# Two-input GpSimd work moved to VectorE, and Strassen sums accumulated in PSUM, in a hybrid SSD and attention layer

## The chip, the cores and the metric

The kernel runs on one core of a Trainium2 chip. Its time is the device time of one execution in microseconds (us). Engines are named as the profile names them: PE (matmul), DVE (VectorE), ACT (ScalarE), POOL (GpSimd) and SP, whose queue issues every DMA.

## The reference

One layer with two token mixers on a sequence of 1024 positions and a width of 1024, in float32. Shortened:

```python
ada = silu(c) @ w_ada + b_ada;  shift, scale, gate = split(ada, 3)
h = rmsnorm(x, norm_w) * (1 + scale) + shift
z_ssm, xbc, dt_raw, q, k, v, z_att, f_logit, g_logit = split(h @ w_in)   # 8472 columns
# SSD branch: 16 heads of 64, 2 groups, state 64, chunks of 128
xbc = silu(causal_conv(xbc, 4 taps));  xs, B, C = split(xbc)
dt = softplus(dt_raw + dt_bias);  a_cs = cumsum(-exp(a_log) * dt)  # inside a chunk
y = ((C B^T) * exp(a_cs[l] - a_cs[s]) masked) @ (xs * dt) + C @ state * exp(a_cs) + d_skip * xs
y_ssm = rmsnorm(y * silu(z_ssm), ssm_norm_w)
# attention branch: 8 heads of 128, causal
p = softmax(q k^T / sqrt(128) + f_cum[query] - f_cum[key]);  y_att = (p @ v) * silu(z_att)
g_ssm, g_att = split(sigmoid(g_logit + b_gate))
merged = g_ssm * (y_ssm @ w_proj_ssm) + g_att * (y_att @ w_proj_att)
out = rmsnorm(x + gate * (merged @ w_out), final_norm_w)
```

## The kernel before

**Split products.** Every float32 matrix A becomes two tiles of a matmul type, Ah (A rounded) and Al = A - Ah, and a product is three matmuls: Ah Bh, Ah Bl and Al Bh. `split` (L101 to L104) makes the pair: ACT casts (L102), then an engine given as an argument subtracts (L103). The default is GpSimd, `G`; some calls give `V`, VectorE. `unit` loads 128 x 512 weights into a tile `wr` and splits them into `wh` and `wl`. Operands called h or hh are high parts, l or hl low parts.

**Stages.** In order of time: normalisation of x, transposed into `hh`, `hl`, with DVE preparing what PE transposes (L261, L263, L302) and making the low part (L307); a first slab of v with the dt and forget columns (`t_slab`, L140 to L142; `tmp`, L348) and `t_forms`, which builds the Strassen forms of h (`tha`, `tla`, `thb`, `tlb`); then the pair stage; the SSD scan; attention; the projections of both branches; the output projection with the final normalisation.

**The pair stage.** `c_pair` computes two slabs of 128 columns of the in-projection at a time, 19 pairs, in Winograd's form of Strassen: sums of the four weight blocks (L476 to L479), seven splits f1 to f7, seven products of 12 matmuls of 512 columns (L495 to L497), each into a PSUM bank of its own from `bank()`, which goes round eight banks (three named `mm`, five `pp`). f1 is copied out (L503), and seven adds on DVE (L504, 505, 507, 508, 511, 514, 517) combine the products with tiles `pe`. What an evac does depends on the slab: `silu_out` (tanh on ACT, L524, then DVE, L525), `conv_out` (a copy, later DVE operations of 1024, L541 to L547), `gate_out` (tanh, L186). `w_sums` (L571 to L592) prepares Strassen sums of the projections' weights between pairs and stores them to `ws_scr`.

**SSD.** `ssd_half` handles four quarters of the heads by eight chunks. Per chunk: the decay matrix `ab` on ACT and DVE with its split into `m`, transposes of `xs` (L691), `xd` (L700), `xe` and their splits into `xr`, the state `sn` with its split, the products (L728, L739, L740) and the sums on DVE (L741). The squares of y collect in `sacc` (L777, L778). The rest of the v and some q and k slabs (L115 to L117, L140 to L142) are handed to the scheduler as work of lower priority.

**After the scan.** `sacc` is summed by PE (L784), raised to -1/2 by GpSimd (L789), transposed (L791). `attend` computes logits (L1012), softmax pieces (L1013 to L1021), transposes and p v; q and k are split in `qk_slab` at 1024 columns, v in `v_load`.

**Projections.** `prod_c` and `post` do each branch's projection in the same seven products, for four blocks p, with DVE adds as in the pairs; `b_form` builds the forms of the data. Three products of the SSD projection run as `early` work during attention. In the output projection `out_pre` (L1126) adds x1, u3 and u4 into the residual on GpSimd, and `out_done` adds the last product, squares, scales and stores. The tables `WV` and `WVI` give the weight splits of some blocks to DVE.

**Order.** A scheduler with a timeline model fixes the order of instructions on each engine when the kernel is built, from the order of the code and the priorities (`APRI`, `SPRI`). At run time every engine takes its own queue in order.

Of the kernel before, what the change touches and what calls it, by code (L numbers as in the profile page):

```python
# [31 lines left out]
P = 128  # L32
# [18 lines left out]
OSSM = (1, 2, 6, 7, 5, 4, 3)  # L51
OATT = (1, 2, 6, 7, 5, 4, 3)
OOUT = (1, 2, 6, 7, 5, 4, 3)
WV = {'ps': (), 'pa': (1,), 'o': (1, 2, 3)}
WVI = (("o", 3),)
# [14 lines left out]
def build(ctx, tc, t):  # L70
# [16 lines left out]
    def unit(src, n, eng=G):  # L87
# [13 lines left out]
    def split(raw, hi, lo, n, eng=G):  # L101
        A.copy(out=hi[:, :n], in_=raw[:, :n])  # L102
        eng.tensor_tensor(out=lo[:, :n], in0=raw[:, :n], in1=f32(hi[:, :n]), op=ALU.subtract)  # L103
        return hi, lo  # L104
# [91 lines left out]
    def w_in(n, i, p):  # L196
        if (n, i, p) in ws_scr:
            return unit(ws_scr[n, i, p], 512, V if p in WV[n] or (n, i) in WVI else G)
        return unit(t["w_" + n][p + 4 * (i == 4), i % 2 == 0 and 1 or 0], 512)
# [160 lines left out]
    with tc.tile_pool(name="pa", bufs=1, side="right") as pa, \  # L360
# [74 lines left out]
        def t_forms(k):  # L435
# [3 lines left out]
            for b, kk, hs, eng in ((b11, k, lo, V), (b12, k, hi, G), (b22, k + 4, hi, G), (b21, k + 4, lo, V)):  # L439
                eng.tensor_tensor(out=b, in0=f32(hh[kk][:, hs]), in1=f32(hl[kk][:, hs]), op=ALU.add)  # L440
# [4 lines left out]
            for b, th, tl, hs, eng in ((b11, th1, tl1, lo, V), (b12, th1, tl1, hi, G), (b22, th2, tl2, hi, V),  # L445
                                       (b21, th2, tl2, lo, G)):
# [12 lines left out]
        def c_pair(sa, sb, evac_a, evac_b):  # L459
# [22 lines left out]
            f6 = s_form(s2)  # L482
            f7 = a_form(a21)
            f5 = s_form(s1)
            f4 = a_form(a22)
            f2 = a_form(a12)
            f3 = s_form(s4)

            def prod(f, xs, k0, hf):
                ps = bank()  # L490
                hs = slice(hf * 512, (hf + 1) * 512)
                for k in range(4):
                    w = slice(k * P, (k + 1) * P)
                    xh, xl = xs[k0 + k]
                    PE.matmul(ps, lhsT=f[0][:, w], rhs=xh[:, hs], start=(k == 0), stop=False)  # L495
                    PE.matmul(ps, lhsT=f[0][:, w], rhs=xl[:, hs], start=False, stop=False)
                    PE.matmul(ps, lhsT=f[1][:, w], rhs=xh[:, hs], start=False, stop=(k == 3))  # L497
# [4 lines left out]
            x1, u2, u3, u4 = pe_tile(), pe_tile(), pe_tile(), pe_tile()  # L502
            A.copy(out=x1, in_=prod(f1, h, 0, 0))  # L503
# [71 lines left out]
        def w_sums(n, p, gb=None):  # L575

            def raw_in(sl, u):
                x = raw_tile()[:, :512]
                SP.dma_start(out=x, in_=t["w_" + n][sl, u])
                if gb is not None:  # L580
                    (V if u else G).tensor_tensor(out=x, in0=x, in1=gb[:, 512 * (sl // 4):512 * (sl // 4) + 512],
# [6 lines left out]
            G.tensor_tensor(out=a21, in0=a11, in1=a21, op=ALU.subtract)  # L588
            G.tensor_tensor(out=s4, in0=a12, in1=s2, op=ALU.subtract)
# [40 lines left out]
    with tc.tile_pool(name="sd", bufs=1, side="right") as sd, \  # L630
# [40 lines left out]
        def ssd_half(qd, hf, xs, ys, st32, sn):  # L671
# [3 lines left out]
            for c in range(4 * hf, 4 * hf + 4):  # L675
# [81 lines left out]
        for qd in range(4):  # L757
            st32, sn = sd.tile([P, 256], F32, tag="st32", bufs=1, name="st32"), None
            for hf in range(2):
# [7 lines left out]
                for i in range(2):  # L767
# [8 lines left out]
                    else:  # L776
                        A.activation(out=zt, in_=y, func=AF.Square)  # L777
                        G.tensor_tensor(out=sacc[:, hs], in0=sacc[:, hs], in1=zt, op=ALU.add)  # L778
# [75 lines left out]
    def b_t2(b11, b12, b22, b21=None):  # L854
# [5 lines left out]
        if b21 is not None:  # L860
            G.tensor_tensor(out=b21, in0=b21, in1=t2, op=ALU.subtract)
        return f

    RESULT = {2: (0, 0), 4: (1, 0), 3: (0, 1)}

    def post(i, p, ps, x, u3, done, pre=None):


        if i == 1:
            x[p] = fin_tile("x1", 4)  # L870
            A.copy(out=x[p], in_=ps)
        elif i == 6:
            V.tensor_tensor(out=x[p], in0=ps, in1=x[p], op=ALU.add)
        elif i in (5, 7):
            if p not in u3:
                u3[p] = fin_tile("u3", 4)
                if i == 5:
                    A.copy(out=u3[p], in_=x[p])
                    V.tensor_tensor(out=x[p], in0=ps, in1=x[p], op=ALU.add)
                else:  # L880
                    V.tensor_tensor(out=u3[p], in0=ps, in1=x[p], op=ALU.add)
                if pre:
                    pre(1, 1, p, (x if i == 5 else u3)[p])
            else:
                y, z = (u3, x) if i == 7 else (x, u3)
                V.tensor_tensor(out=y[p], in0=ps, in1=y[p], op=ALU.add)
                if not pre:
                    V.tensor_tensor(out=ps, in0=ps, in1=z[p], op=ALU.add)
                done(1, 1, p, ps)
        else:  # L890
            if not pre:
                V.tensor_tensor(out=ps, in0=ps, in1=u3[p] if i == 4 else x[p], op=ALU.add)
            done(*RESULT[i], p, ps)
        if pre and i in (1, 5, 7):
            pre(*RESULT[{1: 2, 5: 3, 7: 4}[i]], p, (u3 if i == 7 else x)[p])

    def prod_c(i, n, bf, x, u3, done):

        for p in range(4):
            hi, lo = w_in(n, i, p)  # L900
            ps = bank()
            for k in range(4):
                c = slice(k * P, (k + 1) * P)
                PE.matmul(ps, lhsT=hi[:, c], rhs=bf[k][0], start=(k == 0), stop=False)
                PE.matmul(ps, lhsT=hi[:, c], rhs=bf[k][1], start=False, stop=False)
                PE.matmul(ps, lhsT=lo[:, c], rhs=bf[k][0], start=False, stop=(k == 3))
            post(i, p, ps, x, u3, done)
# [14 lines left out]
    sx, su3 = {}, {}  # L922

    def early(i):

        fs = []
# [5 lines left out]
        for k in range(4):  # L932
            if i == 2:
                e = piece(4 + k, LO)
            elif i == 7:
                e = raw_tile()[:, :512]
                V.tensor_tensor(out=e, in0=ub[22][k], in1=ub[12][k], op=ALU.subtract)
            elif i == 3:
                e = ub[22][k]
            else:  # L940
                e = piece(k, LO)
                for q in {1: (), 5: (12,), 6: (12, 22), 4: (12, 22)}[i]:
                    V.tensor_tensor(out=e, in0=ub[q][k], in1=e, op=ALU.subtract)
                if i == 4:
                    e2 = piece(4 + k, LO)
                    V.tensor_tensor(out=e, in0=e2, in1=e, op=ALU.subtract)
            fs.append(b_split(e))
# [6 lines left out]
        prod_c(i, "ps", fs, sx, su3, done)  # L954

    with tc.tile_pool(name="at", bufs=1, side="right") as at, \
# [97 lines left out]
        for h in range(AH):  # L1054
# [10 lines left out]
            for i in EARLY.get(h, ()):  # L1065
                early(i)
                if i == 1:
# [9 lines left out]
    with tc.tile_pool(name="finp", bufs=1, space=PSUM) as fpp_:  # L1077
# [4 lines left out]
        b = {**ub, **(b_quads(us_scr, (11, 21)) if 4 not in done_early else {})}  # L1082
# [3 lines left out]
        prep_u = 6 in done_early  # L1086
# [154 lines left out]
```

## Time and profile before

| | |
|---|---|
| median of 3 runs | 1287.4 us (1284.27 to 1290.71) |
| the profiled execution | 1286.09 us, span 1284.4 us |
| mean granted PE clock | 0.974 |
| PE | 1183.9 us, 92% of the span, 6206 matmuls |
| DVE | 963.1 us, 75%, 1618 |
| ACT | 594.8 us, 46%, 1194 |
| POOL | 776.1 us, 60%, 644 |
| DMA | 219.70 MB, mean 171 GB/s |

The share of an engine is its busy time over the whole span; stages have different limits, so the prediction reads it by stretches: 0 to 75 us is the start, 75 to 120 the first slab and `t_forms`, 120 to 545 the pair stage, 545 to 770 the SSD scan (its setup until 580), 770 to 1060 attention, 1060 to 1188 the projections, 1188 to 1285 the output projection and its tail.

### The profile page before, as it was taken

The page shows a single profiled execution, that of the slowest core. Times are in us where ns is not written, and L with a number is a line of the kernel's source. Part 1 is how long each engine was busy: PE and PEld are TensorE (multiplying, and loading weights), DVE is VectorE, ACT ScalarE, POOL GpSimd, SP SyncE. Part 2 cuts the span into 40 slices and gives each one's busy share as a digit, 9 for nine tenths or more (in the row PEclk, how much of TensorE's full clock was granted, in tenths as well). Part 3 has the DMA queues.
Part 4 walks back from the last instruction along what each step waited for, and adds up shares of the span by engine and source line. Part 5 has one row for each costly group of instructions (what it writes and reads, how often), then busy time and mean ns, then how long its engine had stood idle before and what let it go on. Part 6 is the DMA issues. An engine that isn't in the chain of part 4 may idle for free. (4 is left out here: it accounts for less than half of the span.)

```text
span 1284.4 us, 18783 instructions
## 1 busy us (share of the span) xinstructions
PE 1183.9 (92%) x6206; PEld 988.8 (77%) x6206; DVE 963.1 (75%) x1618; ACT 594.8 (46%) x1194; POOL 776.1 (60%) x644
## 2 busy tenths in 40 slices
PE   4897899999978999999988999999999999999896
PEld 3686688777766788799778888888887787878685
DVE  6979767787799566348689764545667968999997
ACT  5443324242423232477667733444456553444354
POOL 3258465474755476448887966435446635587666
PEclk9998899998989999999999999999999999999999
DMA  8422443624556566654565558623236619766143
GB/s 346 158 100 98 160 123 124 213 64 167 188 185 216 175 211 228 223 177 148 188 200 163 173 191 296 210 87 116 74 127 210 201 55 328 224 188 193 52 116 145
DMA packets 104126, 219.70 MB, mean 171 GB/s; under 512 B 11818, under 2 KB 19420, under 8 KB 103004
## 3 DMA queue, kind: packets, MB, share of 16 engines
q1 hardware_dynamic: 104028, 218.50, 51.5%
q8 instruction: 49, 0.80, 0.3%
q14 instruction: 49, 0.40, 0.1%
HBM read 154.85 MB, written 63.61 MB: 170 GB/s over the span
## 5 line engine op out<-in xcount | busy, mean ns | idle before, releaser
L103 POOL TENSOR_TENSOR wl<-wr,wh 128x512 fp32r<-128x512 f32 (+1 forms) x188 | 281.5, 1508 | 135.7 <-ACT wh L102 130.7
L102 ACT CAST wh<-wr 128x512 fp32r<-128x512 f32 (+1 forms) x214 | 129.8, 618 | 158.4 <-DMA wr<-w_c 53.7
L103 POOL TENSOR_TENSOR sl<-sr,sh 128x512 fp32r<-128x512 f32 x57 | 91.0, 1603 | 78.8 <-ACT sh L102 65.7
L115 PE MATMUL mm<-hh,wh 128*128 128x512 f32 x288 | 115.9, 407 | 4.3 <-ACT wh L102 1.9
L116 PE MATMUL mm<-hl,wh 128*128 128x512 f32 x288 | 116.7, 405 | 3.0 <-DVE hl L307 3.0
L117 PE MATMUL mm<-hh,wl 128*128 128x512 f32 x288 | 116.3, 405 | 0.0
L102 ACT CAST sh<-sr 128x512 fp32r<-128x512 f32 x57 | 34.1, 619 | 96.6 <-DVE sr L478 77.0
L140 PE MATMUL mm<-wh,hh 128*128 128x256 f32 (+1 forms) x256 | 74.9, 294 | 3.8 <-DVE tmp L348 3.8
L141 PE MATMUL mm<-wl,hh 128*128 128x256 f32 (+1 forms) x256 | 74.8, 293 | 0.0
L142 PE MATMUL mm<-wh,hl 128*128 128x256 f32 (+1 forms) x256 | 74.4, 292 | 0.0
L1018 ACT ACTIVATE pr<-pr,sm 128x1024 f32<-128x1024 f32 (+3 forms) x64 | 49.9, 780 | 50.4 <-DVE sm L1017 42.4
L1021 POOL TENSOR_SCALAR pr<-pr,sm 128x1024 f32<-128x1024 f32 (+3 forms) x64 | 48.6, 762 | 34.7 <-DVE sm L1020 30.2
L1013 DVE CUSTOM_DVE_ANT_0 pr<-lg,fb 128x512 f32<-128x512 f32 (+1 forms) x96 | 51.5, 551 | 23.5 <-PE lg L1012 14.0
L115 PEld LDWEIGHTS mm<-hh,wh 128*128 128x128 f32 x288 | 55.1, 193 | 15.6 <-ACT wh L102 2.4
L116 PEld LDWEIGHTS mm<-hl,wh 128*128 128x128 f32 x288 | 55.3, 192 | 14.7 <-DVE hl L307 3.9
L1004 POOL TENSOR_SCALAR_AFFINE_SELECT fb<-fb 128x128 f32<-128x128 f32 x64 | 21.9, 344 | 72.1 <-DVE sm L1013 57.3
L117 PEld LDWEIGHTS mm<-hh,wl 128*128 128x128 f32 x288 | 55.2, 192 | 10.8
L1037 DVE TENSOR_TENSOR ptl<-tp,pth 128x512 fp32r<-128x512 f32 (+1 forms) x80 | 50.1, 632 | 15.9 <-ACT pth L1036 15.5
L1036 ACT CAST pth<-tp 128x512 fp32r<-128x512 f32 (+1 forms) x80 | 42.3, 543 | 41.5 <-PE tp L1033 32.4
L683 ACT ACTIVATE ab<-ab,acs 128x128 f32<-128x128 f32 x128 | 41.1, 391 | 31.7 <-DMA ab<-a_scr 28.1
L140 PEld LDWEIGHTS mm<-wh,hh 128*128 128x128 f32 x256 | 49.5, 194 | 4.7 <-DVE tmp L348 4.5
L103 POOL TENSOR_TENSOR m<-ab,m 128x512 fp32r<-128x512 f32 x32 | 46.7, 1462 | 7.1 <-ACT m L102 4.7
(393 smaller groups left out, 3972.6 us busy)
## 6 DMA issues: line engine op xcount, KB each, us to landing
wr<-w_c SPq DMA_DIRECT2D x116, 256.0 KB, 3.5
wa<-w_ada SPq DMA_DIRECT2D x8, 1024.0 KB, 11.4
g_scr<-gt SPq DMA_DIRECT2D x16, 512.0 KB, 4.0
ab<-a_scr SPq DMA_DIRECT2D x32, 256.0 KB, 3.7
gt<-g_scr SPq DMA_DIRECT2D x32, 256.0 KB, 3.0
wr<-w_ps SPq DMA_DIRECT2D x28, 256.0 KB, 2.9
wr<-w_pa SPq DMA_DIRECT2D x28, 256.0 KB, 3.1
wr<-so SPq DMA_DIRECT2D x28, 256.0 KB, 2.6
```

The costliest lines, as they stand in the source:

```text
L102: A.copy(out=hi[:, :n], in_=raw[:, :n])
L103: eng.tensor_tensor(out=lo[:, :n], in0=raw[:, :n], in1=f32(hi[:, :n]), op=ALU.subtract)
L115: PE.matmul(ps, lhsT=hi[:, cs], rhs=xh[k][:, hs], start=(k == 0), stop=False)
L116: PE.matmul(ps, lhsT=hi[:, cs], rhs=xl[k][:, hs], start=False, stop=False)
L117: PE.matmul(ps, lhsT=lo[:, cs], rhs=xh[k][:, hs], start=False, stop=(k == 7))
L140: PE.matmul(o, lhsT=xh[k][:, ts], rhs=hi[:, cs], start=(k == 0), stop=False)
L141: PE.matmul(o, lhsT=xh[k][:, ts], rhs=lo[:, cs], start=False, stop=False)
L142: PE.matmul(o, lhsT=xl[k][:, ts], rhs=hi[:, cs], start=False, stop=(k == 7))
L1013: V.tensor_tensor_reduce(out=pr[:, n0:n1], in0=lg[:, :n1 - n0], in1=fb[:, n0:n1], op0=ALU.add, op1=ALU.min, scale=1.0, scalar=BIG, accum_o ...
L1018: A.activation(out=pr[:, :n], in_=pr[:, :n], func=AF.Exp, scale=-1.0, bias=sm[:, 0:1], accum_out=sm[:, 1:2])
L1021: G.tensor_scalar(out=pr[:, :n], in0=pr[:, :n], scalar1=sm[:, 1:2], scalar2=0.5, op0=ALU.mult, op1=ALU.mult)
L1037: V.tensor_tensor(out=ptl[:, :w], in0=tp[:, :w], in1=f32(pth[:, :w]), op=ALU.subtract)
```

## The change

**From GpSimd to VectorE.** Every GpSimd operation with two tensors as inputs is given to DVE: the default engine of `split` and `unit`, and the `G.tensor_tensor` calls of `t_forms`, `w_sums`, `xe`, `sacc`, `b_t2`, `att_done` and `out_done`. GpSimd keeps the powers, `affine_select` and the `tensor_scalar` of the softmax. `WV` and `WVI` go.

**Sums in PSUM.** In `c_pair` a product may be accumulated onto an existing bank: f2 onto f1's, f7 and then f4 onto f6's (after DVE has added x1 in that bank and ACT has copied it out as u2, then as u3), f3 onto f5's. A pair uses three banks, three adds (L505, L512, L513 after the change) and three copies instead of seven, seven and one. In the projections `post` keeps banks in `held`, and `ONTO` names whose bank a product continues; `out_pre` goes. The early products are made per block p, 1 and 2 together, 6 by itself.

```diff
-    def split(raw, hi, lo, n, eng=G):
+    def split(raw, hi, lo, n, eng=V):
...
-                (V if u else G).tensor_tensor(out=x, in0=x, in1=gb[...], op=ALU.mult)
+                V.tensor_tensor(out=x, in0=x, in1=gb[...], op=ALU.mult)
...
-                    G.tensor_tensor(out=h4(xe), in0=h4(xd), in1=hb4(dec), op=ALU.mult)
+                    V.tensor_tensor(out=h4(xe), in0=h4(xd), in1=hb4(dec), op=ALU.mult)
...
-            def prod(f, xs, k0, hf):
-                ps = bank()
+            def prod(f, xs, k0, hf, ps=None):
+                first, ps = ps is None, bank() if ps is None else ps
...
-            A.copy(out=x1, in_=prod(f1, h, 0, 0))
-            V.tensor_tensor(out=u2, in0=prod(f6, ttb, 0, 1), in1=x1, op=ALU.add)
-            V.tensor_tensor(out=u3, in0=prod(f7, tta, 0, 1), in1=u2, op=ALU.add)
-            ps = prod(f5, tta, 0, 0)
-            V.tensor_tensor(out=u4, in0=ps, in1=u2, op=ALU.add)
-            V.tensor_tensor(out=ps, in0=ps, in1=u3, op=ALU.add)
-            evac_b(hi, ps)
-            ps = prod(f4, ttb, 0, 0)
-            V.tensor_tensor(out=ps, in0=ps, in1=u3, op=ALU.add)
-            evac_b(lo, ps)
-            ps = prod(f2, h, 4, 0)
-            V.tensor_tensor(out=ps, in0=ps, in1=x1, op=ALU.add)
-            evac_a(lo, ps)
-            ps = prod(f3, h, 4, 1)
-            V.tensor_tensor(out=ps, in0=ps, in1=u4, op=ALU.add)
-            evac_a(hi, ps)
+            pa_ = prod(f1, h, 0, 0)
+            A.copy(out=x1, in_=pa_)
+            pb = prod(f6, ttb, 0, 1)
+            V.tensor_tensor(out=pb, in0=pb, in1=x1, op=ALU.add)
+            A.copy(out=u2, in_=pb)
+            pd = prod(f5, tta, 0, 0)
+            prod(f7, tta, 0, 1, pb)
+            A.copy(out=u3, in_=pb)
+            prod(f2, h, 4, 0, pa_)
+            evac_a(lo, pa_)
+            V.tensor_tensor(out=c22, in0=pd, in1=u3, op=ALU.add)
+            V.tensor_tensor(out=pd, in0=pd, in1=u2, op=ALU.add)
+            prod(f4, ttb, 0, 0, pb)
+            evac_b(lo, pb)
+            evac_b(hi, c22)
+            prod(f3, h, 4, 1, pd)
+            evac_a(hi, pd)
...
+    ONTO = {2: 1, 7: 6, 4: 6, 3: 5}
...
-            V.tensor_tensor(out=x[p], in0=ps, in1=x[p], op=ALU.add)
+            V.tensor_tensor(out=ps, in0=ps, in1=x[p], op=ALU.add)
+            A.copy(out=x[p], in_=ps)
+            held[6, p] = ps
...
+    def prod_bank(i, p, held):
+        ps = held.get((ONTO.get(i), p))
+        return (bank(), True) if ps is None else (ps, False)
...
-        def out_pre(hf, tk, p, st):
-            r = rt[4 * tk + p, hf]
-            G.tensor_tensor(out=r, in0=r, in1=st, op=ALU.add)
```

The line numbers shift a little: the pair products are L492, L494 and L495 after the change, the logits L1023, `split` L95 to L99, `c_half` L111 to L113.

**Where instructions stand.** First PE's queue from the last chunk of the scan to the first logits, before. `ch`, `cl` and `sn` are the scan's last product, `hh`, `hl` with `wh`, `wl` the matmuls of spilled slabs.

```order
L739 MATMUL sp<-ch_4635,sn 128x128
L740 MATMUL sp<-cl_4637,sn 128x128
L117 MATMUL mm<-hh_238,wl 128x512
L115 MATMUL mm<-hh_231,wh 128x512
...
L784 MATMUL sp<-ones,sacc 128x1 x8
...
L791 MATMUL sp<-ident,rc 8x128
...
L1012 MATMUL lg<-kh,qh 128x512
```

The same place after the change:

```order
L739 MATMUL sp<-ch_4521,sn 128x128
L740 MATMUL sp<-cl_4523,sn 128x128
L784 MATMUL sp<-ones,sacc 128x1 x4
L111 MATMUL mm<-hh_235,wh 128x512
...
L113 MATMUL mm<-hh_238,wl 128x512
L784 MATMUL sp<-ones,sacc 128x1 x4
L791 MATMUL sp<-ident,rc 8x128
L1023 MATMUL lg<-kh,qh 128x512
```

Before, 99 slab matmuls stand between the last L740 and the first logits (49 ahead of L784, 28 behind it, 22 behind L791); after, 12, all between the halves of L784.

Second, PE's queue in the pair stage where one pair's f7 ends, before; the next product, f5, goes to another bank and waits for its split alone.

```order
L495 MATMUL pp<-tha_1134,wh 128x512
L496 MATMUL pp<-tla_1135,wh 128x512
L497 MATMUL pp<-tha_1134,wl 128x512
L495 MATMUL pp<-tha_1062,sh 128x512 [waits DVE_49,Activation_49]
L496 MATMUL pp<-tla_1063,sh 128x512
L497 MATMUL pp<-tha_1062,sl 128x512 [waits Pool_49]
```

The end of f7 in one of the pairs after the change, where f4 follows at once on the same bank:

```order
L492 MATMUL mm<-tha_1134,wh 128x512
L494 MATMUL mm<-tla_1135,wh 128x512
L495 MATMUL mm<-tha_1134,wl 128x512
L492 MATMUL mm<-thb_1064,wh 128x512 [waits Activation_49]
L494 MATMUL mm<-tlb_1065,wh 128x512
L495 MATMUL mm<-thb_1064,wl 128x512 [waits DVE_49]
```

f4's first matmul now has ACT's copy of the bank (u3) ahead of it. In the 19 pairs the matmuls of other products that stand between the end of f7 and the start of f4 are 0, 24, 24, 24, 24, 0, 0, 12, 22, 17, 22, 19, 0, 2, 24, 22, 12, 12 and 19; between f6 and f7, 0 in the first pair and 20 to 74 in the others.

Third, DVE's queue in a pair with a convolution slab, before and after (`cv`, `xp`: the convolution; `sr`, `wr`: weight sums; `pe`, `pp`, `mm`: the products):

```order
L507 TENSOR_TENSOR pe<-pp,pe 128x512
L508 TENSOR_TENSOR pp<-pp,pe 128x512
L544 SCALAR_TENSOR_TENSOR cv<-xp,cv 128x1024
L511 TENSOR_TENSOR pp<-pp,pe 128x512
```

```order
L99 TENSOR_TENSOR wl<-wr,wh 128x512
L512 TENSOR_TENSOR pe<-mm,pe 128x512
L513 TENSOR_TENSOR mm<-mm,pe 128x512
L544 SCALAR_TENSOR_TENSOR cv<-xp,cv 128x1024
L586 TENSOR_TENSOR sr<-wr 128x512
L99 TENSOR_TENSOR sl<-sr,sh 128x512
L505 TENSOR_TENSOR pp<-pp,pe 128x512
```

Behind the change the splits (L99) stand in DVE's queue among the adds, which they did on POOL's before.

More of the change, by code (lines that the diff above doesn't have):

```diff
@@ L871, in post @@
             A.copy(out=x[p], in_=ps)
+            held[1, p] = ps
         elif i == 6:
[L873 to L892 removed]
+            V.tensor_tensor(out=ps, in0=ps, in1=x[p], op=ALU.add)
@@ new lines, in post @@
+            A.copy(out=x[p], in_=ps)
+            held[6, p] = ps
+        elif i == 7:
+            if (6, p) not in held:
+                V.tensor_tensor(out=ps, in0=ps, in1=x[p], op=ALU.add)
+                held[6, p] = ps
+            held["u3", p] = fin_tile("u3", 4)
+            A.copy(out=held["u3", p], in_=ps)
+        elif i == 5:
+            u3 = held.pop(("u3", p))
+            V.tensor_tensor(out=u3, in0=ps, in1=u3, op=ALU.add)
+            V.tensor_tensor(out=ps, in0=ps, in1=x[p], op=ALU.add)
+            held[5, p] = ps
+            done(1, 1, p, u3)
+        else:
@@ L893, in post, with prod_c @@
             done(*RESULT[i], p, ps)
[L894 to L899, printed above, removed]
+    def prod_bank(i, p, held):
+        ps = held.get((ONTO.get(i), p))
+        return (bank(), True) if ps is None else (ps, False)
+    def prod_c(i, n, bf, x, held, done, p=None):
+        for p in range(4) if p is None else (p,):
             hi, lo = w_in(n, i, p)
-            ps = bank()
+            ps, new = prod_bank(i, p, held)
@@ L902, in prod_c @@
             for k in range(4):
                 c = slice(k * P, (k + 1) * P)
[L904 to L907, printed above, removed]
+                PE.matmul(ps, lhsT=hi[:, c], rhs=bf[k][0], start=(new and k == 0), stop=False, skip_group_check=True)
```

146 lines of the change are left out of this document (78 added, 68 removed).

## Prediction

> **What bounds the kernel now.** I read the page first, then the busy time of each engine by stage, then the waits of PE, then single stretches of the timeline. Rows of the stage view: stretch in us, its length, busy us (instructions) of PE, weight loads, DVE, ACT and POOL, the granted clock, DMA share, GB/s.
>
> ```profile
> PE 1183.9 (92%) x6206; PEld 988.8 (77%) x6206; DVE 963.1 (75%) x1618; ACT 594.8 (46%) x1194; POOL 776.1 (60%) x644
> ...
> 0.00:75.00 75.00, 52.01 (x232) 39.91 (x233) 54.68 (x122) 37.49 (x61) 19.19 (x24) 0.98 0.57 216
> 75.00:120.00 45.00, 37.70 (x231) 34.36 (x230) 42.92 (x43) 17.52 (x35) 36.80 (x22) 0.92 0.35 118
> 120.00:545.00 425.00, 396.64 (x1658) 315.77 (x1657) 311.38 (x402) 144.21 (x249) 252.07 (x168) 0.96 0.52 174
> 580.00:770.00 190.00, 176.34 (x1289) 156.84 (x1289) 146.92 (x295) 126.78 (x315) 153.49 (x141) 0.98 0.57 177
> 770.00:960.00 190.00, 189.37 (x1091) 164.79 (x1091) 100.62 (x279) 86.27 (x173) 92.89 (x111) 1.00 0.45 150
> 960.00:1060.00 100.00, 92.69 (x539) 79.15 (x538) 77.92 (x189) 58.09 (x119) 54.94 (x64) 0.97 0.49 158
> 1060.00:1188.00 128.00, 124.33 (x534) 99.87 (x535) 122.59 (x144) 54.29 (x94) 87.83 (x57) 1.00 0.72 234
> 1188.00:1285.00 97.00, 80.30 (x338) 63.82 (x336) 88.35 (x113) 43.53 (x90) 62.76 (x44) 0.95 0.33 104
> ```
>
> PE is the bound. Its idle time by stage (length less busy) is 23.0, 7.3, 28.4, 13.7, 0.6, 7.3, 3.7 and 16.7 us: 101 us, nearly all of the 100.5 that the span has. The matmuls stay as many, so this idle time, and what the clock takes after it, is all that there is to win. After a long wait PE runs at half rate (start, duration):
>
> ```profile
> 373.80 0.39 PE L497 MATMUL mm<-tha,sl 128*128 128x512 f32 x1
> 381.49 0.79 PE L495 MATMUL mm<-thb,wh 128*128 128x512 f32 x1 [7.30 <-ACT gt L186]
> 382.08 0.63 PE L496 MATMUL mm<-tlb,wh 128*128 128x512 f32 x1
> ```
>
> The clock of 0.96 in the 425 us of the pair stage is a loss of about 0.04 x 425 = 17 us beside its 28.4 idle. Whom PE waits for (total us, times, longest):
>
> ```profile
> PE mm L495 <- ACT gt L186: 11.2, 2, 7.3
> PE tp L302 <- DVE xt L263: 7.2, 2, 6.2
> PE mm L495 <- DVE zt L525: 6.8, 1, 6.8
> PE xp L691 <- DVE xd L700: 5.4, 4, 2.6
> PE xp L691 <- DMA xs<-x_scr: 4.7, 5, 1.9
> ...
> PE mm L140 <- DVE tmp L348: 3.8, 3, 3.0
> ...
> PE tp L302 <- DVE rs L261: 3.1, 3, 2.1
> PE mm L116 <- DVE hl L307: 3.0, 2, 2.3
> PE pp L1157 <- DVE wl L103: 2.8, 2, 2.0
> ...
> PE mm L1157 <- POOL wl L103: 2.7, 1, 2.7
> ```
>
> Mostly DVE, hardly POOL. But POOL makes DVE slow:
>
> ```profile
> L103 DVE TENSOR_TENSOR bl<-b,bh 128x512 fp32r<-128x512 f32 x32 | 36.1, 1152 | 0.0
> L892 DVE TENSOR_TENSOR mm<-mm,x 128x512 f32<-128x512 f32 x10 | 6.9, 686 | 0.0
> L103 POOL TENSOR_TENSOR wl<-wr,wh 128x512 fp32r<-128x512 f32 (+1 forms) x188 | 281.5, 1508 | 135.7 <-ACT wh L102 130.7
> ```
>
> ```profile
> 1205.50 5.04 POOL L1126 TENSOR_TENSOR b<-b,x 128x512 f32<-128x512 f32 x3
> 1209.35 1.75 DVE L103 TENSOR_TENSOR wl<-wr,wh 128x512 fp32r<-128x512 f32 x1
> 1217.90 0.68 DVE L103 TENSOR_TENSOR wl<-wr,wh 128x512 fp32r<-128x512 f32 x1
> 1218.51 0.68 DVE L844 TENSOR_TENSOR tt<-m 128x512 f32<-128x512 f32 x1
> ```
>
> The same split takes DVE 1.75 us while POOL works and 0.68 with POOL idle; the next then starts 0.61 after it. With an operand in PSUM it is 0.69 throughout. So a DVE operation with two SBUF inputs waits out a POOL operation.
>
> **The change part by part.** The order counts POOL 649 instructions before and 157 after, DVE 1620 and 1992, ACT 1108 and 1166, PE 6177 both times. Of 492 that leave POOL, 16 vanish (L1126) and 476 come to DVE: 377 of width 512 at 0.60 us, 15 of 1024 at 1.14, 84 of 256 at 0.33 (0.60 less or more the width at about 1.05 ns): 226 + 17 + 28 = 271 us. 104 adds leave DVE (four in each of 19 slab pairs, 28 in the projections): 62 us. Today's 1618 DVE instructions, counted by width at these free spacings, are about 718 us of the 963; the other 245 are lock and pipeline tail. DVE after: 718 + 271 - 62 = 927, up to 990 with the tails of lone operations. Its total hardly moves, while POOL falls to 80 or 90 us. Stage by stage, against the profiled 1286.09 us (span 1284.4; median of the runs 1287.4):
>
> Start, 0 to 75: DVE sets PE here (7.2, 3.1, 3.0). Its free load with the 9 moved splits is 42 + 6 = 48 us against 54.7 busy. I take -5 of the 7; bounds -9 (both sides of the idle share) and 0, since splits now stand in DVE's queue ahead of rows of L263 and wait there for a DMA and a cast.
>
> 75 to 120 (t_forms, dt_chain): DVE is busy 42.9 of 45; free, with 22 moved, 34. The waits on tmp fall away: -5, bounds -10 (idle plus half rate) and 0.
>
> Pair stage: free DVE load 238 + 100 moved - 46 removed = 292 of 425, where it is 311 now, and POOL's 252 are gone. The waits on gt and zt came from heads of in-order queues; they ease, but a DMA can still hold them. Half of the 28.4 and no less of the clock's share would be 14 or more; I take 13. Against it: a product now waits for an add and a copy on its own bank. In the new order most of them have 12 to 74 other matmuls in front (2.8 us and up at 0.23 each); five copies before f4 have none or two, and one f6 to f7 has none. Price by these rows:
>
> ```profile
> L503 ACT COPY pe<-pp 128x512 f32<-128x512 f32 x12 | 7.0, 584 | 2.2 <-PE pp L497 2.2
> 757.02 0.42 DVE L741 TENSOR_TENSOR ys<-sp,eb 128x256 f32<-128x256 f32 x1 [2.89 <-PE sp L740]
> ```
>
> A copy is 0.58, PE's last matmul ends 0.17 after the next could start (0.40 against 0.23), and hand-overs are 0.03 to 0.12: 0.9 us; with the add 1.7. Five times 0.9 plus 1.7 is 6 to 7. Net -6. Bounds: -30 (all idle and some clock) and +30 (19 pairs with 0.9 + 0.7 more at late copies).
>
> SSD, 580 to 770: free load 102 + 64 = 166 of 190 on one queue that today is 147 (DVE) and 153 (POOL) on two. The chain of a chunk is shorter (a split 0.6 instead of POOL's 1.5) and the new order puts 883 filling matmuls between the chunks, before 779. Waits on xd (5.4) ease, those on xs stay: -5; bounds -14 (the idle time) and +11 (below).
>
> End of SSD into attention: those fillers are missing at the end. Between the last chunk (L740) and the first logits (L1012) 99 stand now, 12 after.
>
> ```profile
> 756.71 0.28 PE L740 MATMUL sp<-cl,sn 128*128 128x128 f32 x1
> 759.84 1.28 DVE L773 TENSOR_TENSOR ys<-ys,zt 128x512 f32<-128x512 f32 x2
> 760.60 1.24 ACT L777 ACTIVATE zt<-ys 128x512 f32<-128x512 f32 x2 [2.70 <-DVE ys L773]
> 761.31 2.67 POOL L778 TENSOR_TENSOR sacc<-sacc,zt 128x512 f32<-128x512 f32 x2 [2.60 <-ACT zt L777]
> 770.12 1.05 ACT L102 CAST qh<-qt 128x1024 fp32r<-128x1024 f32 x1 [0.84 <-issue]
> 774.31 2.40 POOL L103 TENSOR_TENSOR kl<-qt,kh 128x1024 fp32r<-128x1024 f32 x1
> 781.72 0.40 PE L1012 MATMUL lg<-kh,qh 128*128 128x512 f32 x1
> ```
>
> Followed with DVE's prices: squares done at 761.8, sacc 762.5, sums L784 (1.8) 764.4, cast 765.5, ql and kl until about 768: 11 us after L740, of which PE has 12 fillers (2.8), the sums and a transpose (2.1). Idle 6, and 1.7 for one half-rate window: +8; bounds 0 and +12.
>
> Attention, 770 to 1060: 26 and 19 splits come to a DVE that is at 53 and 78%; 15 are of 1024 and stand 1.1 us in front of softmax pieces: 0; bounds -3 and +5.
>
> Closing, from 1060: DVE is full now (122.6 of 128, then 88.4 of 97). Free: 86 + 34 and 59 + 22, less 28 adds and the 16 of L1126, is 175 of 225. The waits on wl (2.8 and 2.7) and their like go; in the last projection, whose four banks end together, a product waits up to 1 us for the copies at two seams. -8; bounds -14 and 0. The tail of squares, power and stores behind the last matmul stays.
>
> Sum: -5 -5 -6 -5 +8 +0 -8 = -21, so 1265 for the profiled execution and 1266 against the median.
>
> **A rule against it.** By the trace a DVE operation starts 0.61 us after one that lasts 0.68. The Trainium skill, page "VectorE: DVE Perf Modes", section "The DRAIN you can't avoid", says that the next operation does not start until the pipe is empty. The trace does not agree (1217.90 + 0.68 is later than 1218.51). By that rule the 435 operations of the SSD stage would be an estimated 35 us dearer, 201 in 190 us.
>
> **The rivals.** (a) Slower: PE loses its lead. Today each of seven products of a pair has its own of eight banks, 19 us of run-ahead; afterwards it is one or two products. For it: in-order waits of 7 us exist (gt, zt). Against it: the covers of 2.8 us and more. If late adds cost each of 19 pairs 1.9 us more, 36 us, it ends at 1302; from 1.1 us per pair (21 us) it eats the whole gain.
> (b) No change: the waits are of queue heads and DMA, not of the lock; pair and SSD stages give nothing (+11) and the start and the closing only half (+9): 1286.
> (c) DVE becomes the bound in the SSD stage, where in 600 to 750 it would be filled to some 95%: +11 instead of -5, 1282.
> (d) A larger gain: waits on DVE go nearly all, half-rate windows with them: start -9, 75 to 120 -9, pair -25, SSD -10, transition +4, closing -12: 1226.
>
> **Chances.** Forecast 0.45; (d) or halfway to it 0.22; (c) 0.09; (b) 0.12; (a) 0.12. A change under 0.5% (6.4 us) can hardly be told from none here. Faster (under 1281): 0.41 + 0.22 + 0.04 = 0.67. Same: 0.04 + 0.05 + 0.09 = 0.18. Slower: 0.12 + 0.03 = 0.15. The range goes from 1234, past the middle of (d), to 1299, most of (a); the forecast's own is 1252 to 1280.
>
> **What would show it.** Right: DVE splits near 0.68 everywhere, POOL under 100 us, DVE 930 to 990 busy; fewer half-rate windows before 120; a PE gap of about 6 us before the first logits; PE waits on copies of u3 near 1 us. Wrong: many PE waits on the adds at L505 and L513 of over 2 us, SSD stage with DVE over 95% and longer than now, or a closing that DVE still fills.

## The result, and the profile after

The changed kernel takes 1237.4 us (median of 4, 1229.0 to 1239.91) against 1287.4: a ratio of 0.96, interval 0.9546 to 0.9654. On another chip, in a later run, it was 1235.9 (0.9604, interval 0.9569 to 0.9639). So it gained 50 us where 21 were forecast, in the forecast direction and inside the range. The profiled execution is the shortest of its four, 1229.0, so differences of stages from it sum to 57. A second profile (span 1234.3) puts 2.6 us more into the start, 1.5 into the scan and 2.8 into attention; the pair stage is the same to 0.2 us.

The page's first part, of after:

```profile
PE 1162.5 (95%) x6206; PEld 975.1 (79%) x6206; DVE 969.8 (79%) x1990; ACT 626.2 (51%) x1252; POOL 87.2 (7%) x152
```

PE does the same matmuls in 21.4 us less busy time (1183.9 before) and is idle 64.7 us instead of 100.5. The half-rate windows of the clock fell from 16 to 4 in this profile, and to 9 in the second one of the changed kernel.

Stages begin at other times now. To compare the same work, both traces are cut at the first `t_slab` matmul, the first and last pair product, the first matmul of the scan, the first logits, the last p v product, and the first output product. First before, then after (columns as in the stage view of the prediction):

```profile
0.00:75.90 75.90, 52.91 (x236) 40.63 (x237) 55.48 (x123) 38.39 (x63) 19.44 (x25) 0.98 0.56 214
75.90:120.10 44.20, 36.90 (x227) 33.70 (x226) 42.23 (x42) 16.61 (x33) 36.65 (x23) 0.92 0.36 121
120.10:542.10 422.00, 393.64 (x1633) 312.80 (x1632) 310.39 (x400) 142.28 (x246) 251.97 (x167) 0.96 0.52 173
...
554.00:781.70 227.70, 214.04 (x1572) 192.23 (x1573) 161.02 (x331) 150.08 (x367) 179.16 (x163) 0.99 0.57 180
781.70:1061.20 279.50, 271.40 (x1583) 235.38 (x1581) 177.95 (x464) 138.77 (x285) 138.27 (x168) 0.99 0.44 146
1061.20:1188.10 126.90, 123.39 (x529) 99.10 (x530) 122.24 (x144) 54.39 (x94) 87.83 (x57) 1.00 0.73 236
1188.10:1284.40 96.30, 80.20 (x337) 63.76 (x335) 88.25 (x112) 43.44 (x90) 62.76 (x44) 0.95 0.33 104
```

```profile
0.00:70.80 70.80, 51.85 (x235) 39.89 (x236) 51.70 (x132) 38.35 (x63) 6.14 (x15) 1.00 0.59 229
70.80:108.20 37.40, 37.40 (x248) 35.03 (x247) 36.38 (x69) 18.82 (x38) 0.00 (x0) 1.00 0.50 170
108.20:499.10 390.90, 379.70 (x1641) 305.15 (x1640) 300.19 (x487) 161.34 (x281) 0.00 (x0) 1.00 0.55 186
...
509.70:733.80 224.10, 213.63 (x1573) 190.56 (x1572) 202.79 (x491) 150.10 (x368) 1.65 (x1) 0.99 0.55 179
733.80:1021.30 287.50, 275.63 (x1596) 238.90 (x1596) 197.16 (x509) 143.05 (x291) 74.74 (x128) 0.99 0.44 148
1021.30:1140.00 118.70, 115.64 (x492) 92.19 (x493) 107.46 (x177) 56.61 (x100) 0.00 (x0) 1.00 0.75 248
1140.00:1227.20 87.20, 78.06 (x337) 62.84 (x335) 69.28 (x126) 47.52 (x98) 4.69 (x8) 0.97 0.36 112
```

31 of the 57 us are in the pair stage: 14 us less PE busy time and 17 less idle, with DVE at 300 us of work where it had 310. Some matmuls moved between stages (36 of the projections into attention), so the table gives the loss of a stage. The loss is its length less its matmuls at the spacing at which they follow each other when nothing waits (0.23 us for 512 columns, 0.118 for 256, 0.06 for 128).

| loss, us | before | after | difference | forecast |
|---|---|---|---|---|
| start | 38.2 | 33.1 | -5.1 | -5 |
| first slab, `t_forms` | 11.8 | 0.3 | -11.5 | -5 |
| pair stage | 47.0 | 17.2 | -29.8 | -6 |
| scan and its setup | 34.4 | 21.4 | -13.0 | -5 |
| last chunk to first logits | 1.0 | 7.1 | +6.1 | +8 |
| attention | 39.4 | 44.2 | +4.8 | 0 |
| projections, output, tail | 23.6 | 14.7 | -8.9 | -8 |

Whom PE waits for, after; of the waits on gt and zt (11.2 and 6.8) 2.8 is left, and those on tmp, hl and POOL's wl are gone:

```profile
PE tp L298 <- DVE xt L259: 7.6, 2, 6.2
PE lg L1023 <- DVE sm L1024: 4.7, 5, 2.9
...
PE pv L1054 <- DVE zg L1057: 4.0, 4, 2.2
PE pp L492 <- DVE zt L525: 2.8, 1, 2.8
...
PE mm L492 <- ACT pe L509: 1.6, 2, 1.0
PE pp L492 <- ACT pe L509: 1.6, 2, 1.0
...
PE mm L492 <- ACT pe L506: 1.5, 1, 1.5
...
PE xp L691 <- DVE xd L700: 1.2, 3, 0.5
...
PE mm L492 <- DVE mm L513: 0.6, 1, 0.6
```

The rows of L509, L506 and L513 are the price of sharing banks: a product that waits for the copy of u3 (L509) or u2 (L506), or for an add (L513). Together 5.3 us.

### The profile page after: what moved, and what is told of

The parts are those of the page before. It is cut to its first block, busy times and chain, and to the rows that moved or that the text cites. A ratio compares the mean times of both kernels' runs of the same rounds, so it can differ in the third digit from the quotient of the medians.

```text
span 1227.2 us, 18314 instructions
## 1 busy us (share of the span) xinstructions
PE 1162.5 (95%) x6206; PEld 975.1 (79%) x6206; DVE 969.8 (79%) x1990; ACT 626.2 (51%) x1252; POOL 87.2 (7%) x152
## 4 chain that ended last, share of the span: by engine, by line
PE 71%; DVE 14%; DMA 8%; issue 3%; ACT 3%; POOL 0%; SPq 0%; POOLq 0%; DVEq 0%; ACTq 0%
PE pp L492 6%; PE pp L495 6%; PE pp L494 6%; PE pv L1054 4%; PE mm L492 4%; PE mm L494 4%; PE mm L495 4%; PE lg L1023 3%; PE mm L112 3%; PE mm L111 3%; PE mm L113 3%; DMA ab<-a_scr 2%; PE tp L1044 2%; PE mm L908 2%; PE mm L906 2%
## 5 line engine op out<-in xcount | busy, mean ns | idle before, releaser
L99 DVE TENSOR_TENSOR wl<-wr,wh 128x512 fp32r<-128x512 f32 (+1 forms) x214 | 145.8, 689 | 47.3 <-ACT wh L98 46.1
L111 PE MATMUL mm<-hh,wh 128*128 128x512 f32 x288 | 115.5, 406 | 0.1
L113 PE MATMUL mm<-hh,wl 128*128 128x512 f32 x288 | 114.7, 399 | 0.0
L111 PEld LDWEIGHTS mm<-hh,wh 128*128 128x128 f32 x288 | 54.5, 191 | 10.9 <-ACT hh L302 0.9
L113 PEld LDWEIGHTS mm<-hh,wl 128*128 128x128 f32 x288 | 54.8, 190 | 10.1
L1032 POOL TENSOR_SCALAR pr<-pr,sm 128x1024 f32<-128x1024 f32 (+3 forms) x64 | 52.0, 813 | 83.1 <-DVE sm L1031 65.9
L1054 PE MATMUL pv<-pth,vh 128*128 128x256 f32 (+1 forms) x160 | 45.2, 282 | 4.9 <-DVE zg L1057 4.0
L137 PEld LDWEIGHTS mm<-wl,hh 128*128 128x128 f32 x256 | 48.2, 189 | 0.2
L138 PEld LDWEIGHTS mm<-wh,hl 128*128 128x128 f32 x256 | 48.2, 189 | 0.1
```

The source lines that it names most:

```text
L111: PE.matmul(ps, lhsT=hi[:, cs], rhs=xh[k][:, hs], start=(k == 0), stop=False)
L113: PE.matmul(ps, lhsT=lo[:, cs], rhs=xh[k][:, hs], start=False, stop=(k == 7))
L137: PE.matmul(o, lhsT=xh[k][:, ts], rhs=lo[:, cs], start=False, stop=False)
L138: PE.matmul(o, lhsT=xl[k][:, ts], rhs=hi[:, cs], start=False, stop=(k == 7))
L1054: PE.matmul(pv[:, o0:256], lhsT=x[kb // 4][:, kb % 4, vs], rhs=y[:, d:d + m], start=(kb == 0 and i == 0), stop=(kb == 2 * qq + 1 and i == 2))
```

## The experiments

**The two halves of the change, apart.** `moved_only` is the kernel before with every two-input GpSimd operation on VectorE, and no other edit. Two of its edits:

```diff
-    def split(raw, hi, lo, n, eng=G):
+    def split(raw, hi, lo, n, eng=V):
...
-            G.tensor_tensor(out=r, in0=r, in1=st, op=ALU.add)
+            V.tensor_tensor(out=r, in0=r, in1=st, op=ALU.add)
```

> The kernel before with only the first part of the change: every two-input GpSimd operation (the 16 residual adds of L1126 too) on VectorE, the seven banks and seven adds of a pair and the adds of the projections kept. Theory A (the lock between the two engines was the cost, and PSUM accumulation adds little): 1240 to 1255 us, POOL under 100 us busy, the pair stage within 8 us of the changed kernel's 391. Theory B (fewer banks and fewer adds were what freed PE): 1270 to 1287. Theory C (each part needs the other, since VectorE gets full with 104 adds more, 62 us): 1258 to 1280 with VectorE over 1000 us busy.

`psum_only` is the changed kernel with `eng=G` and every other two-input operation back on GpSimd, `WV` and `WVI` too.

> The changed kernel with every two-input operation back where it stood, on GpSimd: only the accumulation in PSUM is left of the change. Theory A: 1270 to 1295, VectorE's copies of two-SBUF operations still at 1.1 us and more where GpSimd works. Theory B: 1235 to 1250. Theory C: 1265 to 1285.

`moved_and_pairs` is `moved_only` with the changed `c_pair`.

> The operations moved to VectorE and the pairs accumulated in PSUM; the projections add as before (out_pre on VectorE). Against the changed kernel it lacks only the accumulation of the projections, 12 adds and 16 residual adds. Theory A: within 6 us of the changed kernel, 1234 to 1246, the loss after the last attention product only. Theory B: 1237 to 1245. Theory C: 1240 to 1255, since VectorE was full in the projections (122.6 of 128 us before).

| | time, us | ratio to before (interval) | pair stage, us | DVE busy, us |
|---|---|---|---|---|
| before | 1287.3 | | 422.0 | 963.1 |
| psum_only | 1302.1 | 1.0116 (1.0092 to 1.0141) | 429.2 | 877.1 |
| moved_only | 1248.6 | 0.9709 (0.9681 to 0.9737) | 398.0 | 1040.3 |
| moved_and_pairs | 1241.9 | 0.9652 (0.9625 to 0.9678) | 392.2 | 994.2 |
| changed | 1237.4 | 0.96 (0.9546 to 0.9654) | 390.9 | 969.8 |

`moved_only` came out in theory A's range; `psum_only` is slower than all three theories allowed, and `moved_and_pairs` lies in the range of each. Theory A holds for the direction: moving alone gains 39 us, accumulating alone loses 15. But the halves don't add up, and there theory C saw something: accumulation costs 15 where GpSimd splits and gains 11 where VectorE does. The pair stage of `psum_only`, then of `moved_only`, and the waits of PE in `psum_only`:

```profile
120.20:549.40 429.20, 396.83 (x1633) 313.13 (x1632) 261.33 (x325) 161.84 (x285) 249.55 (x167) 0.96 0.51 169
```

```profile
109.80:507.80 398.00, 379.29 (x1613) 302.97 (x1612) 344.23 (x563) 141.19 (x243) 0.00 (x0) 0.98 0.52 180
```

```profile
PE pp L494 <- ACT pe L511: 5.5, 3, 2.8
...
PE mm L494 <- ACT pe L511: 3.8, 2, 3.1
```

In `psum_only` DVE has 261 us of work in 429, so 49 us less work there (310.39 before) buys nothing, and sharing banks costs its waits: 11.7 us of PE's time behind copies and 3.9 behind adds, the longest 3.1. In `moved_only` DVE works 344 of 398, and the 44 us that accumulation takes from it (300.19 after) are worth 7 us of the stage. In this profile nearly all of that is one place, where the sums `gb` of the gate's weights (L561) stand on DVE. From 355 to 381 us DVE works 25.96 of the 26.00 us, then waits 0.98 and 0.49 us for loads of `wga`, and PE waits twice:

```profile
PE mm L495 <- DVE zt L525: 6.7, 1, 6.7
PE pp L570 <- DVE gb L561: 5.2, 1, 5.2
```

Behind these waits PE runs at half rate for 17 us. After the change the same place costs a wait of 2.8 on zt and 3.4 us of half rate.

One thing differs between all these builds and stands in no edit: the scheduler makes a new order for each. Between the last chunk and the first logits the traces have 99 slab matmuls before, 130 in `psum_only`, 24 in `moved_only` and 12 after. No run holds the order fixed, so the price of an edit here is its price with the order that comes with it.

**Where on GpSimd does the cost come from?** The first trial added spare GpSimd work to the changed kernel, behind each weight piece (`jo` is read by nobody):

```diff
+    def spare(raw):
+        for i in range(4):
+            r = raw[:, i * 112:(i + 1) * 112]
+            G.tensor_tensor(out=jo, in0=r, in1=r, op=ALU.subtract)
```

> The changed kernel, and behind the load of each of the 245 weight pieces that are split, four spare GpSimd subtractions with two SBUF inputs, 112 wide, into a tile that nobody reads. No engine waits for them except the buffer of the raw piece. Theory A (two-input work on GpSimd makes VectorE wait, wherever it stands): 1262 to 1300 us, VectorE's split of 512 at a mean over 0.85 us, VectorE over 1060 us busy. Theory D (the loss before came from GpSimd's own slow splits of 1.5 us in the chain to PE, not from the lock): 1230 to 1245.

For `spare_one_input` the loop runs eight times over `G.tensor_scalar(out=jo, in0=r, scalar1=1.0, scalar2=0.5, ...)`.

> As the kernel with spare subtractions, with eight spare GpSimd operations of one input (multiplied by two constants) in the place of the four of two inputs, so about as much GpSimd time. Theory A: as the changed kernel, 1230 to 1245, VectorE's split near 0.69. A rival (any GpSimd work slows VectorE, through the memory they share): as far up as with two inputs, over 1260. Theory D: 1230 to 1245.

1327.5 and 1497.1 us (ratios 1.0307 and 1.1636). The first is above the range of every theory; the second is so too, but for the rival, whose range was open above, and it is far from "as far up as with two inputs". (The traces have 267 pieces, not 245.) The trial tells little of the lock, since small operations are dear (547 ns and 394 ns in the mean for 112 columns) and GpSimd fell behind; as I read it, the raw buffers that it read then came free late. DVE's split of 512 rose only to 781 and 734 ns, while PE waited for casts whose load was late, as in this row of the two-input kernel:

```profile
PE pp L501 <- ACT wh L104: 13.6, 3, 7.8
```

**Splits on GpSimd, in forms.** The better trial puts only the default splits back on GpSimd, every other line stays as changed. `splits_on_pool_two_input` does the true subtraction. The others write zeros as low parts, so they leave out what the low parts add to a product, by other operations of the same place and size:

```diff
-        eng.tensor_tensor(out=lo[:, :n], in0=raw[:, :n], in1=f32(hi[:, :n]), op=ALU.subtract)
+        G.tensor_scalar(out=lo[:, :n], in0=f32(hi[:, :n]), scalar1=1.0, scalar2=0.0, op0=ALU.mult, op1=ALU.mult)
```

> The changed kernel with the low parts of all default splits (weights, pairs, m, xe, sn, q, k, v) made on GpSimd by an operation with one input (times 1, times 0), so the low parts are zero and GpSimd's latency is back in the chain without a two-input operation. Theory A: within 10 us of the changed kernel, 1228 to 1248, VectorE about 230 us less busy. Theory D: 1252 to 1285, since the splits stand in GpSimd's in-order queue again.

> The changed kernel with the default splits alone back on GpSimd, as true subtractions of two SBUF inputs; all other two-input operations stay on VectorE. It differs from the kernel with one-input splits (1212.7) in the form of that operation. Theory A (the two-input form makes VectorE wait): 1262 to 1300 us, VectorE's two-SBUF operations of 512 over 1.0 us in the mean. Theory D (time in GpSimd's queue, 1.5 us against 0.78): the same 1262 to 1300 but also for the kernel that doubles the one-input operation.

> The kernel with one-input splits on GpSimd (low parts zero), the one-input operation issued twice, so that GpSimd takes about the 1.5 us of the two-input one, with no two-input operation on it. Theory A: 1212 to 1235 us. Theory D: 1255 to 1295, near the kernel with true subtractions. Between them: both count, by the distance to the two.

`two_input_on_high_part` and `two_input_on_raw` subtract the high part, or the raw tile, from itself; `one_input_on_both_parts` runs the one-input operation first over the high part, then over the raw tile.

> The kernel with one-input splits on GpSimd, with that operation replaced by the high part minus itself: two SBUF inputs, low parts still zero, and still without reading the raw tile (so the raw buffer comes free as early as with one input). Theory A (the two-input form makes VectorE wait): 1265 to 1295 us, as the true splits on GpSimd (1283.4). Theory E (the true splits held the raw buffers longer, so loads came late): 1225 to 1245, as the doubled one-input operation (1233.8).

> The kernel with the doubled one-input operation, the first over the high part, the second over the raw tile, so that GpSimd holds the raw buffer to its end as the true subtraction does; low parts zero. Theory A: 1228 to 1245 us. Theory E: 1265 to 1290.

> As the kernel that subtracts the high part from itself on GpSimd, but the raw tile from itself: two SBUF inputs, low parts zero, and the raw buffer held until GpSimd has done. If the costs add up (0.35 us of time for each us that VectorE gets busier, as between the one-input and the high-part kernel, 26 for 74, and 12 for the held raw buffer, as between the two doubled one-input kernels): 1245 to 1256 us. If holding the raw buffer under a two-input operation is what makes the true subtraction dear: 1270 to 1288. If neither the held buffer nor this counts: 1234 to 1243, and the 45 us between the high-part kernel and the true subtraction belong to its two different operands.

| low part made by | held | time, us | ratio to before (interval) | GpSimd per split, us | DVE busy, us |
|---|---|---|---|---|---|
| GpSimd, one input | high | 1212.7 | 0.9425 (0.9398 to 0.9452) | 0.78 | 792.4 |
| the same twice | high | 1233.8 | 0.9594 (0.955 to 0.9638) | 2 x 0.79 | 844.8 |
| two inputs, one tile | high | 1238.5 | 0.9629 (0.959 to 0.9668) | 1.22 | 866.2 |
| one input twice | both | 1245.3 | 0.9679 (0.9653 to 0.9706) | 2 x 0.77 | 836.0 |
| two inputs, one tile | raw | 1249.0 | 0.9721 (0.9676 to 0.9766) | 1.21 | 861.0 |
| two inputs, two tiles (true) | both | 1283.4 | 0.9971 (0.9946 to 0.9995) | 1.53 | 910.8 |
| VectorE (the changed kernel) | none | 1237.4 | 0.96 (0.9546 to 0.9654) | | 969.8 |

"Held" is which tiles GpSimd must have read before their buffers come free. The place of the splits, with the order that comes with it, is worth 46 us of the 50. None of the pure theories survives. That GpSimd's time in its queue decides (D) is refuted by the doubled operation: 1233.8, where D had 1255 to 1295. That the two-input form decides (A) is refuted by the high part taken from itself: 1238.5, where A had 1265 to 1295. That the raw buffer decides (E) is refuted by `one_input_on_both_parts`, 12 us dearer and not 50. The kernel with one input was faster than any theory had it, and 25 us faster than with the splits on VectorE. So GpSimd is not a dear place as such, though this kernel leaves out the low parts. The sum that I had written down for `two_input_on_raw` (1245 to 1256) held at 1249.0.

The cleanest pair is `one_input_on_both_parts` against the true subtraction: the same tiles held, the same 1.53 to 1.55 us of GpSimd per split, and 38 us between them. VectorE's busy time differs by 75 us. My reading is that what counts is for how long at a time VectorE is shut out. The waits fit it: in the scan of the true one PE waits 16.0 us for xd and st, which VectorE makes, and 3.3 for GpSimd; in `one_input_on_both_parts` it is 1.5 and 12.3. The zeros do not speed PE up (matmuls of 512 columns follow each other after 0.23 us in both), and the piece of order counted above is nearly the same (143 and 141 slab matmuls, against 12 in the changed kernel). But elsewhere the two orders differ, and no run takes that apart. Three rows from the scan: DVE in the true one, POOL beside it, and the same split on DVE in the kernel with one input, where POOL is idle at that moment:

```profile
601.31 1.50 DVE L99 TENSOR_TENSOR xr<-xd,xr 128x256 fp32r<-128x256 f32 x1
```

```profile
601.10 1.43 POOL L99 TENSOR_TENSOR m<-ab,m 128x512 fp32r<-128x512 f32 x1
```

```profile
602.62 0.42 DVE L102 TENSOR_TENSOR xr<-xd,xr 128x256 fp32r<-128x256 f32 x1
```

The split of 256 takes DVE 0.42 us alone. Started 0.21 us after GpSimd's 1.43, it ends 0.28 us after GpSimd's end (602.81 against 602.53).

**Cover at the end of the scan.** `k5_in_attention` takes one slab out of the scan's filling work, as below; `k7_in_scan` puts one more in, `("k", 7)` at the end of `SPILL` and its number 10 at the end of `FILL`:

```diff
-SPILL = (("q", 0), ("k", 0), ("k", 2), ("k", 4), ("q", 7), ("k", 5), ("k", 6), )
-FILL = [[], [0, 2], [4, 5, 9], [1, 3, 6, 7, 8]]
+SPILL = (("q", 0), ("k", 0), ("k", 2), ("k", 4), ("q", 7), ("k", 6), )
+FILL = [[], [0, 2], [4, 5, 8], [1, 3, 6, 7]]
```

> The changed kernel with one slab (k of head 5, 48 matmuls) no longer computed in the scan and spilled, but in attention. In the new order no filling matmul stands between the last chunk and the first logits, where 12 do. If the transition's loss is set by the chain of sums (my term of +8): the transition stays at 11 to 12 us and the scan gets 9 to 11 shorter. If attention lacks cover (it loses 44 us), it grows by less than the 11 us of the slab: 1228 to 1236. If the scan lacks cover for want of the slab: 1240 to 1250.

> The changed kernel with one more slab (k of head 7, 48 matmuls) computed in the scan and spilled. Taking one slab out of the scan left the scan as long and made attention longer by the slab's 11 us. If filling work is free in the scan: attention 9 to 12 us shorter, the scan 3 to 8 longer, 1229 to 1235. If the scan is full now: 1236 to 1242.

1246.2 and 1237.4 us, against 1235.9 for `changed_again` beside the second:

> The changed kernel as it stands, beside the other runs on the same chip: 1232 to 1240 us.

| us | changed (two profiles) | k5 in attention | k7 in scan |
|---|---|---|---|
| first matmul of the scan to the last | 213.2, 214.7 | 216.0 | 217.3 |
| from there to the first logits | 10.9 | 11.3 | 21.0 |
| attention | 287.5, 290.3 | 299.3 | 279.4 |

Of what I had written down for `k5_in_attention`, the transition held, the shorter scan did not, and the time is in the range for a scan that lacks cover; `k7_in_scan` is in the range for a full scan. With less to fill, the scan is no shorter and the transition as long: that fits a chain of chunks and sums that sets both, as my term of +8 had it for the transition. With more to fill, what attention gains (8 to 11 us) the transition gives back (10).

**Attention.** `attention_splits_on_pool` gives GpSimd the 15 splits of 1024 again (`split(qt, hi, lo, S, G)`, `split(vt, vh[g], vl[g], 4, G)`).

> The changed kernel with the splits of q, k and v at the width of 1024 back on GpSimd, 15 of them, nearly all in attention. There the kernels with the splits on VectorE lose 44 to 50 us of PE's time and those with them on GpSimd 36 to 42. If the 1024-wide splits stand in front of the softmax on VectorE (my term of 0 with +5 as its bound): attention 3 to 7 us shorter, 1229 to 1234. If the small splits for the early projections or the lock cost as much: 1234 to 1240.

1243.1 us (0.9652, interval 0.9628 to 0.9675): above both ranges and slower than the changed kernel, attention 297.7 us against 287.5 and 290.3. My guess falls: these splits don't cost attention its 5 us, and on GpSimd attention is longer still.

## Why the prediction was right or wrong

**Right, by the trace.** The bound and the direction; the start (-5.1 for -5), the transition (+6.1 for +8), the closing stages (-8.9 for -8). DVE's total stayed (969.8, forecast 927 to 990), POOL's came to 87.2 (80 to 90). The lock is gone from DVE's rows, here the scan's multiplication of two SBUF tiles before and after, and the splits at VectorE's price:

```profile
L686 DVE TENSOR_TENSOR ab<-ab,cb 128x512 f32<-128x512 f32 x32 | 33.5, 1051 | 15.1 <-ACT ab L685 12.5 <-POOL sn L103 2.3
```

```profile
L99 DVE TENSOR_TENSOR wl<-wr,wh 128x512 fp32r<-128x512 f32 (+1 forms) x214 | 145.8, 689 | 47.3 <-ACT wh L98 46.1
...
L686 DVE TENSOR_TENSOR ab<-ab,cb 128x512 f32<-128x512 f32 x32 | 21.9, 686 | 2.9 <-ACT ab L685 2.5
```

The transition went as worked out as far as the sums. The last chunk's L740, the squares, sacc, the sums, the power on POOL, the transpose and the first logits:

```profile
722.59 0.28 PE L740 MATMUL sp<-cl,sn 128*128 128x128 f32 x1
...
726.58 1.23 ACT L777 ACTIVATE zt<-ys 128x512 f32<-128x512 f32 x2 [5.49 <-DVE ys L773]
727.25 1.49 DVE L778 TENSOR_TENSOR sacc<-sacc,zt 128x512 f32<-128x512 f32 x2
...
728.79 1.05 PE L784 MATMUL sp<-ones,sacc 128*128 128x1 f32 x8 [2.18 <-DVE sacc L778]
730.12 1.65 POOL L789 TENSOR_TENSOR rc<-rc,mhalf 128x8 f32<-128x8 f32 x1 [703.91 <-DVE rc L787]
731.82 0.38 PE L791 MATMUL sp<-ident,rc 128*8 128x128 f32 x1 [1.99 <-POOL rc L789]
733.80 0.77 PE L1023 MATMUL lg<-kh,qh 128*128 128x512 f32 x1 [1.60 <-DMA fb<-f_scr]
```

11.2 us from L740 to the logits where I had 11. That the total agrees so well is in part luck: I let the cast and the splits of k end it, and it was the power, the transpose and a load.

**Wrong: the pair stage, -6 for -30,** which is at the bound that I had given. Two steps failed. The first is the 13 us taken as "half of the 28.4 and no less of the clock's share". Nothing in the trace said half; it was a middle between bounds. `moved_only` measures that term alone: the stage is 24.0 us shorter and, since it holds 20 matmuls fewer, loses about 19 less. The second is the +7 for late copies, added as if it stood by itself. The price was near (5.3 us of waits after), but the 76 adds that accumulation takes from DVE are worth more once DVE does the splits. The same edit costs 7.2 us with GpSimd splitting (429.2 against 422.0) and gains 7 without (390.9 against 398.0; about 10 by the loss). I had counted those adds in DVE's total, and nothing for them in the sum.

Of the waits that I had put down to in-order queues and DMA, the larger went with the move: in `moved_only` that on gt is 0.6, where it was 11.2. One on zt did not go with it: 6.7 there (6.8 before), 2.8 once accumulation was added. So, as far as one profile of each tells, the operations on GpSimd were behind the first, and the full queue of DVE and a load behind the second, as I had it. Seven half-rate windows stood in this stage before and one after.

**Wrong: the first slab, -5 for -11.5,** beyond its bound of -10: the idle time and the half rate after it went entirely (0.3 us of loss). `moved_only` has the same 37.4 us, so it is the move. **The scan, -5 for -13:** DVE carries 202.8 of 224.1 us there, near the 166 of 190 forecast, and the stage still gained. Rival (c) saw the load right and its effect wrong. The waits on xd eased as I had it (5.4 to 1.2), but those on xs, which I had said would stay, are gone too (4.7 before, 2.1 in `moved_only`, none over 0.2 after). That the chain of a chunk got shorter is my reading; no run shows it apart.

**Attention, 0 for +4.8,** at its bound of +5. The changed kernel, `moved_only` and `moved_and_pairs` lose 44 to 50 us there, the kernels with all default splits on GpSimd 36 to 42. In the changed kernel PE waits 8.7 us there for sm and zg, which DVE makes, and 1.6 before. What held DVE up stays open: the splits of 1024 that I suspected are cleared.

**The rivals.** (a) is refuted for the changed kernel: no product waits over 1.5 us for a copy and 0.6 for an add. Where GpSimd keeps the splits, its mechanism is there: in `psum_only` PE waits 15.6 us for copies and adds. (b) is wrong, since the pair stage and the scan gained most, though waits at the heads of queues were there, as zt shows. What happened is nearest to (d), to which I gave 0.22: its sum was -61, with -25 for the pairs, -10 for the scan and -9 for the first slab, against a profiled -57. In part it is near by luck: of the -30 in the pairs some 10 come from accumulation, which (d) does not name. The evidence for it was in my own quoted rows (1.75 us against 0.68 for the same split, and PE waiting mostly on DVE), and I halved it out of caution.

**The rule against it.** In the output projection after, too, a DVE operation starts before the last has ended:

```profile
1183.49 0.69 DVE L99 TENSOR_TENSOR bl<-m,bh 128x512 fp32r<-128x512 f32 x1 [7.11 <-ACT bh L98]
1184.10 0.69 DVE L99 TENSOR_TENSOR wl<-wr,wh 128x512 fp32r<-128x512 f32 x1
```

So the spacing of 0.60 to 0.61 was the right price. But I had quoted only half of the rule: the Trainium skill, page "VectorE: DVE Perf Modes", section "The DRAIN you can't avoid", adds that a next operation which is not held starts earlier. With that the trace agrees.

## What to carry to other kernels

Before a middle value is taken for a stall, ask what the stall's releasers have in common: here GpSimd's two-input operations lengthened DVE's, DVE was behind most of PE's waits, and most of the stall went at once. Two edits whose effects meet on one engine are not priced apart: in the pair stage, work taken from DVE was worth nothing while DVE had room (261 us of 429) and something once the other edit had filled it (344 of 398). A 2 x 2 of builds shows it in two runs. And where a scheduler makes the order, an edit brings a new order with it: read that first, as the transition's 99 and 12 matmuls show.

## What the runs showed of the hardware

The delay that GpSimd gives a VectorE operation of two SBUF inputs grows with the length of the GpSimd operation, and one input is enough to cause it, which my first theory denied. VectorE's 512-wide operation takes 0.685 us alone. At the 95th percentile (one in twenty takes longer) it takes 1.09 beside the one-input operation (0.62 us where that runs undisturbed), 1.52 beside the two-input one on a single tile (1.04) and 1.78 beside the true subtraction (about 1.30). The delays, 0.41, 0.84 and 1.10, are in each case close to the GpSimd operation less 0.20 us. The Trainium skill, page "SBUF — State Buffer", section "Who interferes with whom", says that a VectorE instruction with two SBUF inputs contends with a GpSimd instruction that reads SBUF, and calls the shared ports an exclusive lock. The trace agrees, but for those 0.20 us.

GpSimd's two-input operation over one tile twice is faster (1.04 us) than over two tiles (1.30). At equal GpSimd time per split, the kernel with the true subtraction keeps VectorE busy 75 us longer than the one with two one-input halves and takes 38 us more; how much of the 38 is the difference in order stays open.
